# One more scheduling step in the S5 loop of a hybrid SSD / S5 / attention layer, and a higher pace for S5's steps

## The chip, the cores and the metric

The kernel runs on one core of one Trainium2 chip. The metric is the device time of one execution in microseconds (us). The kernel before took 1111.87 us, the median of three runs (1111.23, 1111.87 and 1114.11).

## The reference

One inference step of a layer with three branches. A prompt group (16 learned tokens and 512 prompt tokens) and a sample group (64 tokens on top of a cache of 512) go through the same weights. Cut to what matters:

```python
h = rmsnorm(x, norm_mix)                       # D_MODEL = 1024
y_a = ssd_branch(h @ w_z, h @ w_xbc, h @ w_dt) # conv, chunked scan, gate, group norm
y_b = s5_branch(h @ w_u)                       # complex diagonal scan, 32 groups x 64 states
glu = gelu(y_b) @ w_glu
out_b = glu[..., :1024] * sigmoid(glu[..., 1024:])
o_c = stick_breaking(rmsnorm(q), rmsnorm(k), v)
gates = sigmoid(h @ w_gate)                    # three gates of 1024 columns
mix = gates[0] * (y_a @ w_lift_a) + gates[1] * out_b + gates[2] * (o_c @ w_lift_c)
x = x + mix @ w_out
x = x + square(relu(rmsnorm(x) @ w_up)) @ w_down
```

In `s5_branch` the input of every group is mapped to complex states, a recurrence with a fixed complex factor runs over time, and the states are mapped back. The kernel does this in blocks of eight steps: products of powers of the factor with B (`ba_r`, `ba_i`), their product with C (`psk`, later the table `tz`), one scan over blocks, and a second product.

## The kernel before, in words

All large products are dense matmuls in three passes (L336 to L338: high part by high part, high by low, low by high), 128 weights wide, on column halves of 288 or 296. `dense()` walks the weight tiles one after another: for each half it takes one PSUM tile `ps_d`, issues its matmuls and evacuates it. Which engine evacuates depends on the product. In the stretch of `w_glu` (`ybx` is gelu(y_b)) each of eight tiles m has four halves: two of the gate, whose sigmoid ACT writes to `gls` (DVE multiplies it into `gt`), and two of the value, which DVE multiplies into `mix`. A half has 12 matmuls here and 24 in the other products. The weights come by DMA (`w_raw`) and are split by ACT into `w_hi` and by DVE into `w_lo`.

The smaller work (S5, attention, SSD) is written as generators, and each `yield` ends a step. After every half `side(kt)` adds the pace of the first generator in the list, times kt/8, to `credit`; for every whole credit it traces one step. When a generator ends, the next one goes on with the credit that is left:

```python
PACE = {"s5_parts": 1.25, "s5": 1.35, "attention": 1.8, "ssd": 1.1}
        def side(kt):
            credit[0] += pulls[0][1] * kt / 8 if pulls else 0.0
            while credit[0] >= 1.0:
                credit[0] -= 1.0
                pull()
```

The instructions of a step keep their traced order on each of DVE, ACT, POOL and TensorE (`in_order`), while the evacuations and weight splits have a raised priority. A scheduler with a timeline of its own then sets the final order of each engine, and also which PSUM slot a tile gets, and so whose reader it has to wait for.

S5 goes through a loop over q, eight times, with three steps each: `cmul` of `ba_r` and `ba_i` on DVE and POOL; then TensorE transposes them into `ps_r` (L764), adds to `psk` (L765), and ACT copies `ps_r` to `rr`; then `ps_bs` (L775) and the products `mo` on DVE. Behind the loop `kd` is made of `psk`, goes to memory (`kd_scr`, L797) and comes back as `tz` (L834), with which TensorE makes `ps_y` (L847). After S5 comes attention, then SSD, whose chunks c = 1 to 5 are worked on beside `w_glu`: `decay` (an exponential `a` on ACT, L1270; 16 small subtractions on DVE, L1272; an exponential `ar` on ACT, L1273), `weigh` (`ar` times `cb` on DVE), `outputs` (`ps_y`, 32 matmuls, L1318), `state` (`ps_st`, L1293), `turned` (`ps_bt`, `ps_x`), `gather` and `gated`. The sigmoid and the exponential belong to different tables of ACT, so that ACT loads a table (ACT_TABLE_LOAD) whenever it goes from one to the other.

Of the kernel before, what the change touches and what calls it, by code (L numbers as in the profile page):

```python
# [31 lines left out]
LEAD = 120  # L32
WARM = 14
SPLITS = 3
PACE = {"s5_parts": 1.25, "s5": 1.35, "attention": 1.8, "ssd": 1.1}
BUFS = {"ea": 3, "eb": 4, "ec": 3}

PA = {}
# [23 lines left out]
def mixed():  # L62
    n = dict.fromkeys("xzabc", 0)
    out = []
    for c in ORDER:
        out.append(({"x": "xbc", "z": "z", "a": "g1", "b": "g2", "c": "g0"}[c], n[c]))
        n[c] += 1
    return out
# [108 lines left out]
def body(tc, io):  # L177
# [6 lines left out]
    with ExitStack() as ctx:  # L184
# [31 lines left out]
        def tt(e, o, a, b, op):  # L216
            e.tensor_tensor(o, a, b, op=op)  # L217

        def cmul(e, p, shape, orr, oi, ar, ai, br, bi):
            n = 1  # L220
            for x in shape[1:]:
                n *= x
            t = []
            e = e if isinstance(e, tuple) else (e, e)
            for j in range(4):
                g = e[j // 2] is G
                x = p.tile([128, 256], F32, name="cm%d" % j, tag="cm%s%d" % (g, j))[:, :n]
                if len(shape) == 3:
                    x = x.rearrange("p (a b) -> p a b", b=shape[2])
                if len(shape) == 4:  # L230
                    x = x.rearrange("p (a b c) -> p a b c", b=shape[2], c=shape[3])
                t.append(x)
            tt(e[0], t[0], ar, br, OP.mult)
            tt(e[0], t[1], ai, bi, OP.mult)
            tt(e[1], t[2], ar, bi, OP.mult)
            tt(e[1], t[3], ai, br, OP.mult)
            tt(e[0], orr, t[0], t[1], OP.subtract)
            tt(e[1], oi, t[2], t[3], OP.add)
# [210 lines left out]
        def behind(ins, gen):  # L449

            while True:
                with tc.issue_after(ins):
                    if next(gen, done) is done:
                        return
                yield
# [70 lines left out]
        def do_qk(name, m, g, dst, parts):  # L526
            qs = etile("qs", "ea")
            sq = etile("qsq", "eb")
            sh = etile("qsh", "eb", dt=F32R)
            sl = etile("qsl", "ec", dt=F32R)  # L530
            rq = etile("rq", "ec")

            def evac(cols, ps):
                n = cols.stop - cols.start
                copied(cols, ps, qs)
                S.activation(sq[:, cols], ps, AF.Square)
                split(sq[:, cols], sh[:, cols], sl[:, cols])
                pn = psg.tile([128, 512], F32, name="ps_q", tag="g")
                PE.matmul(pn[:, :n], blkr, sh[:, cols], start=True, stop=False)
                PE.matmul(pn[:, :n], blkr, sl[:, cols], start=False, stop=True)  # L540
                rstd_of(ev, pn[:, :n], 64, rq[:, cols], n, "rs")
            dense((name, m), hh, hl, evac, parts=parts)
            c = slice(parts[0].start, T)
            V.scalar_tensor_tensor(qs[:, c], qs[:, c], g, rq[:, c], op0=OP.mult, op1=OP.mult)
            SP.dma_start(dst[m, :, c], qs[:, c])
# [43 lines left out]
        def do_dt():  # L589
            for cols in halves:  # L590
                ps = psd.tile([128, 512], F32, name="ps_dt", tag="d")
                p = ps[:32, :H]
                for k in range(8):
                    PE.matmul(p, w2[:, 0, k, :], hh[:, k, cols], start=k == 0, stop=False)
                    PE.matmul(p, w2[:, 1, k, :], hl[:, k, cols], start=False, stop=k == 7)
                S.activation(dtr[:, cols], p, AF.Copy)
# [123 lines left out]
        def s5():  # L720
# [30 lines left out]
            for q in range(8):  # L751
                ba_r = sp.tile([128, 2, 8, 16], F32, name="ba_r", tag="ba_r%d" % (q % 2))
                ba_i = sp.tile([128, 2, 8, 16], F32, name="ba_i", tag="ba_i%d" % (q % 2))
                sh = [128, 2, 8, 16]
                tq = slice(2 * q, 2 * q + 2)
                P = lambda x: x[:, 7::-1, tq].rearrange("p s t -> p t s").unsqueeze(3).to_broadcast(sh)
                BB = lambda x: x[:, tq, :].unsqueeze(2).to_broadcast(sh)
                cmul((V, G), sp, sh, ba_r, ba_i, P(pr), P(pi), BB(bb_r), BB(bb_i))
                yield
                ps = psg.tile([128, 512], F32, name="ps_r", tag="g")  # L760
                for t in range(2):
                    tq = 2 * q + t
                    for j, (ba, cd) in enumerate(((ba_r, cd_r), (ba_i, cd_i))):
                        PE.transpose(ps[:, 256 * j + 128 * t:256 * j + 128 * t + 128], fs(ba[:, t]), ident)  # L764
                        PE.matmul(psk[:, 32 * tq:32 * tq + 32], fs(ba[:, t]), fs(cd[:, tq]), start=j == 0, stop=j == 1,  # L765
                                  skip_group_check=True)
                rr = sp.tile([128, 512], F32, name="rr", tag="rr%d" % (q % 2))
                S.activation(rr, ps, AF.Copy)
                yield
                z = psg.tile([128, 512], F32, name="ps_bs", tag="g")  # L770
                for t in range(2):
                    for j in range(2):
                        for gl in range(2):
                            c0 = 256 * j + 128 * t + 64 * gl
                            PE.matmul(z[64 * gl:64 * gl + 64, (2 * j + t) * NX:(2 * j + t + 1) * NX],  # L775
                                      rr[:, c0:c0 + 64], ub[:, 2 * (2 * q + t) + gl, :],
                                      start=True, stop=True, skip_group_check=True)
                v3 = lambda x: x.rearrange("p (t b) -> p t b", b=NX)
                zr, zi = v3(z[:, 0:2 * NX]), v3(z[:, 2 * NX:4 * NX])
                ts = slice(2 * q, 2 * q + 2)  # L780
                er, ei = em_r[:, ts, :], em_i[:, ts, :]
                m = [sp.tile([128, 2, NX], F32, name="mo%d" % j, tag="mo%d" % j) for j in range(4)]
                tt(V, m[0], zr, er, OP.mult)
                tt(V, m[1], zi, ei, OP.mult)
                tt(V, m[2], zi, er, OP.mult)
                tt(V, m[3], zr, ei, OP.mult)
                tt(G, d_r[:, ts, :], m[0], m[1], OP.add)
                tt(G, d_i[:, ts, :], m[2], m[3], OP.subtract)
                yield
# [626 lines left out]

        pulls.append((behind(last.ins, s5_parts()), PACE["s5_parts"]))
        for m in range(4):
# [4 lines left out]
        n1.release()  # L1423
        do_dt()
        pulls.append((s5(), PACE["s5"]))
        for m in range(4):
            do_qk("q", m, qg, q_scr, live)
            do_v(m)
            do_qk("k", m, kg, io["k_out"], halves)
        pulls.append((attention(), PACE["attention"]))  # L1430
        for n, m in mixed():
            if n == "xbc":
                do_xbc(m)
                if m == 9:
                    pulls.append((ssd(), PACE["ssd"]))
            elif n == "z":
# [225 lines left out]
```

## Time and profile before

| what | value |
|---|---|
| median of three runs | 1111.87 us (1111.23 to 1114.11) |
| the profiled execution, its own time | 1113.19 us |
| its span | 1111.5 us |
| granted clock, mean over the span | 0.998 |
| TensorE matmul busy | 1095.5 us, 99% |
| TensorE weight load busy | 1056.3 us, 95% |
| VectorE busy | 795.7 us, 72% |
| ScalarE busy | 540.7 us, 49% |
| GpSimd busy | 125.4 us, 11% |

The span is what the profiler saw of the program; the profiled execution's own time has 1.7 us around it. Names: PE is TensorE, PEld its weight loads, DVE is VectorE, ACT ScalarE, POOL GpSimd, SPq the DMA queue of SyncE. L336 is line 336 of the kernel. A row of a timeline gives the start, the duration, the engine, the line, the operation, what it wrote and read, and how many such instructions the row holds; in brackets stands the idle time of the engine ahead of it and what ended that.

### The profile page before, as it was taken

The page shows a single profiled execution, that of the slowest core. Times are in us where ns is not written, and L with a number is a line of the kernel's source. Part 1 is how long each engine was busy: PE and PEld are TensorE (multiplying, and loading weights), DVE is VectorE, ACT ScalarE, POOL GpSimd, SP SyncE. Part 2 cuts the span into 40 slices and gives each one's busy share as a digit, 9 for nine tenths or more (in the row PEclk, how much of TensorE's full clock was granted, in tenths as well). Part 3 has the DMA queues.
Part 4 walks back from the last instruction along what each step waited for, and adds up shares of the span by engine and source line. Part 5 has one row for each costly group of instructions (what it writes and reads, how often), then busy time and mean ns, then how long its engine had stood idle before and what let it go on. Part 6 is the DMA issues. An engine that isn't in the chain of part 4 may idle for free.

```text
span 1111.5 us, 21286 instructions
## 1 busy us (share of the span) xinstructions
PE 1095.5 (99%) x8532; PEld 1056.3 (95%) x8532; DVE 795.7 (72%) x1390; ACT 540.7 (49%) x928; POOL 125.4 (11%) x193
## 2 busy tenths in 40 slices
PE   9999999999999999999999999999999999999998
PEld 8998999999998999897888999999999999999998
DVE  7968579965767466468989754477867776786787
ACT  6465466633365545365657333354444444444443
POOL 1087233011000000021310001200000000000000
PEclk9999999999999999999999999999999999999999
DMA  7653223566754353187445533222232223123222
GB/s 274 149 138 114 94 80 132 136 190 171 222 178 151 112 169 136 64 267 247 133 139 178 173 109 115 99 76 77 76 114 80 74 84 123 60 77 133 77 82 80
DMA packets 80594, 144.04 MB, mean 130 GB/s; under 512 B 26512, under 2 KB 40688, under 8 KB 79984
## 3 DMA queue, kind: packets, MB, share of 16 engines
q1 hardware_dynamic: 80496, 142.69, 41.7%
q8 instruction: 67, 1.10, 0.4%
q14 instruction: 31, 0.25, 0.1%
HBM read 117.40 MB, written 24.38 MB: 128 GB/s over the span
## 4 chain that ended last, share of the span: by engine, by line
PE 83%; DVE 8%; ACT 3%; POOL 2%; issue 2%; DMA 2%; SPq 1%; POOLq 0%; ACTq 0%; DVEq 0%
PE ps_d L336 19%; PE ps_d L337 19%; PE ps_d L338 18%; PE ps_x L1581 3%; PE ps_x L1580 3%; PE ps_x L1582 3%; PE ps_o L895 2%; PE ps_z L895 2%; PE ps_y L1581 1%; PE ps_y L1580 1%; PE ps_y L1582 1%; PE ps_y L1318 1%; DVE w_lo L217 1%; DVE ya L217 1%; PE ps_z L1581 1%
## 5 line engine op out<-in xcount | busy, mean ns | idle before, releaser
L253 ACT ACTIVATE w_hi<-w_raw 128x1024 fp32r<-128x1024 f32 (+1 forms) x150 | 151.9, 1012 | 219.8 <-PE ps_d L337 142.2
L336 PE MATMUL ps_d<-hh,w_hi 128*128 128x288 f32 (+1 forms) x864 | 258.2, 299 | 0.0
L337 PE MATMUL ps_d<-hl,w_hi 128*128 128x288 f32 (+1 forms) x864 | 258.0, 299 | 0.0
L338 PE MATMUL ps_d<-hh,w_lo 128*128 128x288 f32 (+1 forms) x864 | 258.0, 299 | 0.0
L217 DVE TENSOR_TENSOR w_lo<-w_raw,w_hi 128x1024 fp32r<-128x1024 f32 (+1 forms) x150 | 180.3, 1202 | 95.2 <-ACT w_hi L253 91.9
L337 PEld LDWEIGHTS ps_d<-hl,w_hi 128*128 128x128 f32 x864 | 162.6, 188 | 0.9 <-issue 0.3
L338 PEld LDWEIGHTS ps_d<-hh,w_lo 128*128 128x128 f32 x864 | 162.6, 188 | 0.6
L336 PEld LDWEIGHTS ps_d<-hh,w_hi 128*128 128x128 f32 x864 | 162.7, 188 | 0.2
L336 PE MATMUL ps_d<-x2h,w_hi 128*128 128x288 f32 x512 | 151.2, 296 | 0.0
L337 PE MATMUL ps_d<-x2l,w_hi 128*128 128x288 f32 x512 | 151.1, 295 | 0.0
L338 PE MATMUL ps_d<-x2h,w_lo 128*128 128x288 f32 x512 | 150.3, 295 | 0.0
L336 PEld LDWEIGHTS ps_d<-x2h,w_hi 128*128 128x128 f32 x512 | 96.2, 188 | 0.1
L338 PEld LDWEIGHTS ps_d<-x2h,w_lo 128*128 128x128 f32 x512 | 96.2, 188 | 0.1
L337 PEld LDWEIGHTS ps_d<-x2l,w_hi 128*128 128x128 f32 x512 | 96.2, 188 | 0.0
L253 ACT ACTIVATE w_hi<-ws 128x1024 fp32r<-128x1024 f32 x32 | 34.0, 1061 | 55.0 <-PE ps_y L1581 21.6
L1581 PE MATMUL ps_x<-ftl,w_hi 128*128 128x288 f32 x192 | 56.7, 295 | 0.5 <-DVE ftl L217 0.5
L1580 PE MATMUL ps_x<-fth,w_hi 128*128 128x288 f32 x192 | 56.8, 296 | 0.2 <-ACT s L1600 0.2
L1582 PE MATMUL ps_x<-fth,w_lo 128*128 128x288 f32 x192 | 56.4, 294 | 0.0
L1531 ACT ACTIVATE fr<-ps_d 128x288 f32<-128x288 f32 x64 | 25.7, 402 | 55.8 <-PE ps_d L338 55.8
L217 DVE TENSOR_TENSOR w_lo<-ws,w_hi 128x1024 fp32r<-128x1024 f32 x32 | 39.1, 1220 | 12.6 <-ACT w_hi L253 12.6
L336 PE MATMUL ps_d<-ybx,w_hi 128*128 128x288 f32 x128 | 39.7, 310 | 3.0 <-DVE mix L217 2.3
L906 DVE TENSOR_TENSOR_SCAN aw<-col,aw 128x400 f32<-128x400 f32 (+4 forms) x36 | 30.7, 898 | 16.6 <-ACT aw L250 16.6
(471 smaller groups left out, 2643.3 us busy)
## 6 DMA issues: line engine op xcount, KB each, us to landing
w_raw<-wts SPq DMA_DIRECT2D x150, 512.0 KB, 3.5
g_scr<-go SPq DMA_DIRECT2D x24, 288.0 KB, 2.8
gt<-g_scr SPq DMA_DIRECT2D x24, 288.0 KB, 3.0
ar<-ac_scr SPq DMA_DIRECT2D x4, 1024.0 KB, 7.5
x_scr<-cs SPq DMA_DIRECT2D x10, 297.5 KB, 3.1
xc<-x_scr SPq DMA_DIRECT2D x4, 640.0 KB, 7.4
xt<-xT SPq DMA_DIRECT2D x8, 296.0 KB, 5.6
z_scr<-zs SPq DMA_DIRECT2D x8, 288.0 KB, 5.0
```

What stands on the lines that cost most here:

```text
L217: e.tensor_tensor(o, a, b, op=op)
L253: S.activation(hi, x, AF.Copy)
L336: PE.matmul(ps, wh[:, c], xh[:, k, cols], start=start and k == 0, stop=False)
L337: PE.matmul(ps, wh[:, c], xl[:, k, cols], start=False, stop=False)
L338: PE.matmul(ps, wl[:, c], xh[:, k, cols], start=False, stop=stop and k == kt - 1)
L895: mm = lambda *a, **b: PE.matmul(*a, skip_group_check=True, **b)
L906: V.tensor_tensor_scan(x, one.to_broadcast([128, n]), x, 1.0, op0=OP.mult, op1=OP.mult)
L1318: PE.matmul(py[oo, 128 * (h // 2):128 * (h // 2) + n], a, b, start=step == 0, stop=step == 1, skip_group_check=True)
L1531: S.activation(r[:, cols], ps, AF.Relu)
L1580: PE.matmul(ps, w[0][:, o], fh[:, k], start=first and k == 0, stop=False, skip_group_check=True)
L1581: PE.matmul(ps, w[0][:, o], fl[:, k], start=False, stop=False, skip_group_check=True)
L1582: PE.matmul(ps, w[1][:, o], fh[:, k], start=False, stop=k == 3, skip_group_check=True)
```

## The change

The pace of S5's steps goes from 1.35 to 1.53, and a bare `yield` is added in the loop over q, between `cmul` and the transposes. A loop body has four steps instead of three, and S5 has 68 steps instead of 60. All lines from 760 on are one further down after the change.

```diff
-PACE = {"s5_parts": 1.25, "s5": 1.35, "attention": 1.8, "ssd": 1.1}
+PACE = {"s5_parts": 1.25, "s5": 1.53, "attention": 1.8, "ssd": 1.1}
...
                 cmul((V, G), sp, sh, ba_r, ba_i, P(pr), P(pi), BB(bb_r), BB(bb_i))
                 yield
+                yield
                 ps = psg.tile([128, 512], F32, name="ps_r", tag="g")
```

68/60 is 1.133, as is 1.53/1.35, so that S5's last step is traced at the same `side` call as before, and attention's steps are too. The credit left over is another one, by which three steps of SSD are traced one half earlier: the ninth (outputs and state of chunk 1), the twentieth (decay of chunk 5 and the first `gated`) and the thirty-first. The order of the engines differs in the S5 stretch, a little in attention's, and in the stretch of `w_glu`; from the `w_out` product on it is the same.

On ACT in the stretch of `w_glu`, from the first exponential of chunk 4 (`a_6029`) on, the order before was:

```order
L1270 ACTIVATE a_6029<-ar 64x1024 x2
L250 ACT_TABLE_LOAD
L250 ACTIVATE gls<-ps_d 128x288 x2
L253 ACTIVATE w_hi<-w_raw 128x1024
L250 ACTIVATE gls<-ps_d 128x288
L1273 ACT_TABLE_LOAD
L1273 ACTIVATE ar<-ar 128x2048
L1240 ACTIVATE bt<-ps_bt 64x128
L250 ACT_TABLE_LOAD
L250 ACTIVATE gls<-ps_d 128x288
```

At the same place on ACT after the change:

```order
L1271 ACTIVATE a_6029<-ar 64x1024 x2
L250 ACT_TABLE_LOAD
L250 ACTIVATE gls<-ps_d 128x288 x2
L1274 ACT_TABLE_LOAD
L1274 ACTIVATE ar<-ar 128x2048
L253 ACTIVATE w_hi<-w_raw 128x1024
L250 ACT_TABLE_LOAD
L250 ACTIVATE gls<-ps_d 128x288 x2
L1241 ACTIVATE bt<-ps_bt 64x128
```

The first `gls` of tile m = 3 stood ahead of the long exponential `ar`; now the exponential, the weight split `w_hi` and a table load stand ahead of it.

On TensorE the two gate halves of that tile m = 3 are `ps_d_7100` and `ps_d_7115` (names with their numbers). Before, the output block of chunk 3 (`ps_y_6076`, with `ps_st` and `ps_bt` behind it) stood between them:

```order
L336 MATMUL ps_d_7100<-ybx_3296,w_hi_6960 128x288
L337 MATMUL ps_d_7100<-ybx_3296,w_hi_6960 128x288
L338 MATMUL ps_d_7100<-ybx_3296,w_lo_6961 128x288
L1318 MATMUL ps_y_6076<-ar_5724,xd_5766 64x128 x4
L1318 MATMUL ps_y_6076<-a2_5816,st_5899 64x128 x4
```

After the change the second half follows the first at once, and the block stands behind it:

```order
L336 MATMUL ps_d_7100<-ybx_3296,w_hi_6960 128x288
L337 MATMUL ps_d_7100<-ybx_3296,w_hi_6960 128x288
L338 MATMUL ps_d_7100<-ybx_3296,w_lo_6961 128x288
L336 MATMUL ps_d_7115<-ybx_3296,w_hi_6960 128x288
L337 MATMUL ps_d_7115<-ybx_3296,w_hi_6960 128x288
L338 MATMUL ps_d_7115<-ybx_3296,w_lo_6961 128x288
```

In both programs `ps_d_7115` waits for the reader of `ps_d_7100`, the first `gls` of the tile.

On DVE, a little further on, before the change (`a_6243` belongs to the last chunk of decay, `mix` to the values of m = 3):

```order
L217 TENSOR_TENSOR cb<-ps_bt,cst 64x64 x2
L217 TENSOR_TENSOR gt<-gt,gls 128x288
L1272 TENSOR_SCALAR ar<-ar,acm 64x64 x16
L217 TENSOR_TENSOR a_6243<-a_6243,xc 128x8x64
L217 TENSOR_TENSOR ya<-ya,zl 128x288 x2
L217 TENSOR_TENSOR mix<-ps_d,gt 128x288
L217 TENSOR_TENSOR xd<-ps_x,dt 64x512 x2
L217 TENSOR_TENSOR ar<-ar,cb 128x1024 x2
```

And after it (the same last chunk is `a_6209` there):

```order
L217 TENSOR_TENSOR cb<-ps_bt,cst 64x64 x2
L217 TENSOR_TENSOR st<-st,bd 128x512
L217 TENSOR_TENSOR mix<-ps_d,gt 128x288 x2
L217 TENSOR_TENSOR xd<-ps_x,dt 64x512 x2
L217 TENSOR_TENSOR ar<-ar,cb 128x1024 x2
L1273 TENSOR_SCALAR ar<-ar,acm 64x64 x16
L217 TENSOR_TENSOR a_6209<-a_6209,xc 128x8x64
L217 TENSOR_TENSOR ya<-ya,zl 128x288 x2
```

The two `mix` stand ahead of the 16 small subtractions of the last chunk now, and behind them before.

## Rows read from the trace of the kernel before

**Rows 1.** The page: busy time and share of each engine; the chain's shares.
```profile
PE 1095.5 (99%) x8532; PEld 1056.3 (95%) x8532; DVE 795.7 (72%) x1390; ACT 540.7 (49%) x928; POOL 125.4 (11%) x193
...
PE 83%; DVE 8%; ACT 3%; POOL 2%; issue 2%; DMA 2%; SPq 1%; POOLq 0%; ACTq 0%; DVEq 0%
```

**Rows 2.** Waits of TensorE: us in total, times, the longest.
```profile
PE ps_d L336 <- DVE mix L217: 2.3, 3, 1.9
...
PE ps_d L336 <- DVE gt L217: 1.0, 1, 1.0
...
PE ps_ac L1184 <- DVE dta L217: 0.8, 1, 0.8
PE ps_r L764 <- POOL ba_i L217: 0.8, 1, 0.8
PE ps_n L408 <- DVE sa L217: 0.7, 2, 0.5
PE ps_d L336 <- ACT gls L250: 0.6, 1, 0.6
```

**Rows 3.** Windows: length, busy time (x instructions), clock, DMA share, GB/s.
```profile
110.00:217.00 107.00, 107.00 (x866) 104.47 (x866) 85.05 (x123) 62.99 (x141) 29.42 (x46) 1.00 0.36 109
...
515.00:535.00 20.00, 19.38 (x178) 16.39 (x176) 18.79 (x44) 14.31 (x14) 4.22 (x3) 1.00 0.54 169
535.00:555.00 20.00, 18.12 (x164) 15.02 (x163) 18.45 (x48) 13.92 (x18) 5.79 (x4) 0.98 0.39 113
...
554.04:557.45 3.41, 3.41 (x16) 3.41 (x16) 3.41 (x5) 1.89 (x4) 0.00 (x0) 0.50 0.16 44
```

**Rows 4.** Timeline, S5's last block product to the first use of tz.
```profile
190.39 0.75 PE L775 MATMUL ps_bs<-ub,rr 128*64 128x76 f32 x16
...
192.86 0.69 DVE L217 TENSOR_TENSOR kd<-psk,pb 128x512 f32<-128x512 f32 x1
...
193.57 4.06 SPq L797 DMA_DIRECT2D kd_scr<-kd  x8
200.59 7.34 SPq L834 DMA_DIRECT2D tz<-kd_scr  x16
...
206.24 0.34 PE L847 MATMUL ps_y<-ub,tz 128*128 128x73 f32 x2
```

**Rows 5.** Timeline of TensorE at the end of attention.
```profile
303.98 0.43 PE L1184 MATMUL ps_ac<-dta,cst 128*128 128x96 f32 x2 [0.81 <-DVE dta L217]
```

**Rows 6.** Timeline of ACT around the second exponential of chunk 4.
```profile
535.10 0.71 ACT L250 ACTIVATE gls<-ps_d 128x288 f32<-128x288 f32 x2
537.33 1.06 ACT L253 ACTIVATE w_hi<-w_raw 128x1024 fp32r<-128x1024 f32 x1 [1.52 <-PE ps_d L337]
539.05 0.41 ACT L250 ACTIVATE gls<-ps_d 128x288 f32<-128x288 f32 x1 [0.66 <-PE ps_d L338]
540.03 1.28 ACT L1273 ACT_TABLE_LOAD   x1 [0.57 <-DVE ar L1272]
541.33 1.91 ACT L1273 ACTIVATE ar<-ar 128x2048 f32<-128x2048 f32 x1
```

**Rows 7.** Timeline of TensorE: chunk 3's output block and the halves behind it.
```profile
538.95 0.71 PE L1318 MATMUL ps_y<-ar,xd 128*64 128x128 f32 x8
...
544.37 0.40 PE L336 MATMUL ps_d<-ybx,w_hi 128*128 128x288 f32 x1
...
553.75 0.40 PE L336 MATMUL ps_d<-ybx,w_hi 128*128 128x288 f32 x1 [1.88 <-DVE mix L217]
```

**Rows 8.** Timeline of DVE in the same stretch.
```profile
536.82 2.35 DVE L217 TENSOR_TENSOR ar<-ar,cb 128x1024 f32<-128x1024 f32 x2
539.08 0.87 DVE L1272 TENSOR_SCALAR ar<-ar,acm 128x128 f32<-128x128 f32 x4
...
548.65 3.34 DVE L1272 TENSOR_SCALAR ar<-ar,acm 64x64 f32<-64x64 f32 x16 [1.49 <-ACT a L1270]
...
553.26 0.44 DVE L217 TENSOR_TENSOR mix<-ps_d,gt 128x288 f32<-128x288 f32 x1
```

## The prediction, made before the change was timed

> **What bounds the kernel now.** I read the page's shares and its chain first, then the list of TensorE's waits, then windows over the stretches that the change moves, and last the timeline of single instructions there. The reader is to see in the shares that TensorE is busy 1095.5 of 1111.5 us and that the chain runs over it for 83% [rows 1]: 16 us of idle are all that any reordering can win. In the list of waits, no single place has more than 1.9 us [rows 2]. In the windows, the stretch of S5's loop from 110 to 217 us has TensorE busy for 107.00 of 107.00 us, so that nothing can be won there, whatever DVE and POOL do beside it [rows 3]. The one S5 wait in the list, 0.8 us for `ba_i`, lies before that stretch. The second half of the list is the stretch of `w_glu` and SSD: from 515 to 535 us DVE is busy 18.79 of 20 us, from 535 to 555 us 18.45, and TensorE falls to 18.12 there; right behind its longest wait the granted clock is 0.50, the lower level of 1.2 GHz, for 3.41 us [rows 3]. So the change has to be judged where S5 is not: in attention's end and in SSD, whose steps shift by a half.
>
> **The change part by part.** The sums go against the profiled execution's own time, 1113.19 us; the median of the runs shown is 1111.87, so 1.32 us come off at the end.
>
> The bare yield costs no instruction. It only moves the transposes and everything behind them in a loop body to later calls of `side`, while the higher pace brings them forward; a body took 3 steps / 1.35 = 2.22 halves and takes 4 / 1.53 = 2.61. TensorE's matmuls of S5 are the same ones, inserted at other places into a stream that was full. I take 0 for them. Bounds: a wait like the one for `ba_i`, 0.8 us [rows 2], once more or once less. That wait itself stays, since the order of TensorE is the same up to its place.
>
> The later part of the chain of S5 gets a little tighter. From the start of the last `ps_bs`, at 190.39, over `kd` (192.86), its way to memory (from 193.57) and the reload (from 200.59) to the first `ps_y` at 206.24 it is 15.9 us, and TensorE had no gap there [rows 3, 4]. By the order, both ends move forward by about two halves, and the distance on TensorE is some 4.5 halves where it was 4.6, about 15.5 us by the trace's pace; 15.9 - 15.5 makes a wait of 0.4 us. The instruction behind it on SP's queue is the store of the convolution's rows, which nothing waits for soon. Bounds: 0, if the reload's first transfer lands early, and 2, if the 7.34 us in which SPq issues its sixteen parts [rows 4] fall behind a weight load. I take 0.3.
>
> At attention's end TensorE waits 0.81 us for `dta` [rows 5]. In the changed order `ps_ac` stands 0.13 halves later, some 0.4 us, and the DVE chain ahead of it no later. I take -0.5, with bounds of -0.8 and 0.
>
> Now SSD. First, the 0.6 us that TensorE waits for `gls` [rows 2] lie at a place where ACT does `w_hi` ahead of an exponential; after the change it does it behind, one `w_hi` of 1.06 us [rows 6] less ahead of that `gls`. I take -0.5, bounds -0.6 and 0.
>
> Second, and the largest term: TensorE finished the first gate half of tile m = 3 when chunk 3's block began, at 538.95 us, and went on with the second half at 544.37 [rows 7]. That half needs the PSUM tile that `gls` reads, at 539.05 to 539.46 [rows 6]; 5.42 us of `ps_y`, `ps_st` and `ps_bt` hid it. After the change nothing lies between the halves, and on ACT a long exponential, a `w_hi` and two table loads stand ahead of that `gls`. How late is it? The exponential waits for the 16 subtractions of chunk 4 on DVE. They ended at 539.95 before [rows 8]; now the two products `ar<-ar,cb` (2.35 us) and one `xd` (some 0.6) come behind them, so they end at about 537.0. Then, with the durations of [rows 6], a table load 1.30, the exponential 1.91, `w_hi` 1.06, a table load 1.30, `gls` 0.41: 5.98 us, so TensorE goes on at about 543.0. It comes to this place 0.5 earlier than before by the term above, at 538.45. The wait is 543.0 - 538.45, some 4.5 us. The block now runs behind the second half, where it hides nothing that waits. I take +4.5. Bounds: +0.6, the wait for `gls` in the list [rows 2], and +5.4, if the subtractions end where they ended before but for the `xd` and one of the two products (0.87 us later than I reckon, the length of their last four [rows 8]).
>
> Here a page of the Trainium skill speaks. The trace shows that a table load of 1.28 us at 540.03 is followed by the exponential at 541.33, without a gap [rows 6]. The Trainium skill (ScalarE: Activation LUTs, section "What ACT_TABLE_LOAD costs") gives 1283 ns for the load, as this trace does, and about 1380 ns of a drain with every switch to another set. With that, two switches ahead of `gls` would make the wait 2.8 us longer and the sum as much higher; the row shows no such drain ahead of the exponential, so I follow the row.
>
> Third, the clock. A wait of 1.88 us is followed by 3.41 us at the lower level, [rows 3, 7]; half of that, 1.7, is lost. The waits of 0.8 to 1.0 us have no such price: the mean clock of the span, 0.998, is 2.2 us short of full speed in all, and this place alone makes 1.7 of it. A wait of 4.5 us is taken to bring the same as that of 1.88: +1.7, bounds 0 and 1.7.
>
> Fourth, the longest wait goes: 1.88 us for `mix` [rows 7]. There DVE had the 16 subtractions of the last chunk (3.34 us, itself held up 1.49 us by ACT) ahead of `mix` [rows 8]; after the change both `mix` stand ahead of the 16. With TensorE some 4 us later at that place, `mix` is there in time. The wait goes and its stretch at the lower clock too: -1.9 - 1.7 = -3.6. Bounds -3.6 and 0. What is late next is the 16 subtractions themselves, for which the last, small block waits; it comes several halves later.
>
> Fifth, behind it stand three waits for DVE: 1.0 for `gt`, 0.7 for `sa` and the rest of `mix`, 0.4, 2.1 us in all [rows 2]. There DVE is the bound, and its work is the same. If TensorE comes to them later, they shrink by as much. The loss so far in this stretch is -0.5 + 4.5 + 1.7 - 3.6 = +2.1; I take half of the waits, -1.0, bounds -2.1 and +1.0 (a `ps_n` is issued earlier in relation to `sa` in the new order).
>
> Sum: 0.3 - 0.5 - 0.5 + 4.5 + 1.7 - 3.6 - 1.0 = +0.9, so 1114.1 for the profiled execution and 1112.8 for the median. Less than 0.3%, 3.3 us, is what a measurement of this kernel cannot tell from no change, and this is a quarter of it.
>
> **The rivals.**
> *The new wait is not paid back: slower.* Place: the second gate half of m = 3. If `gls` is late by 4.5 us there, the `gt` product on DVE behind it is, too, and in a strict queue all that DVE has behind it: `mix`, `ya`, the state. The DVE windows have only 1.2 and 1.55 us of idle in 20 [rows 3], so what DVE loses there it does not win back, and TensorE waits for `mix` again. Then the term of -3.6 is missing and that of -1.0 too: +0.9 + 4.6 = +5.5, so 1117.4. It decides from the point where DVE idles more than some 2 us at that `gt`; less than that and `w_lo` and `ar<-ar,cb` fill the time. For it speaks how full DVE is, against it that these products now stand exactly ahead of the `gt`. By the drain of the Trainium skill's page this case would come nearer.
> *The new wait is short: faster.* If the exponential has been done before TensorE arrives (the subtractions end earlier, or the scheduler's order leaves ACT free), the wait is 0.6 like the other one for `gls` [rows 2], without a fall of the clock. Then 0.3 - 0.5 - 0.5 + 0.6 - 3.6 = -3.7 with nothing back from the waits behind; with half of them, 1.0, it is -4.7, so 1107.2. Against it: the exponential alone takes 1.91 us, and it can't start before the subtractions.
> *It does for S5 what its words suggest: it takes the waits for `ba_i` away.* That would be -0.8 in the sum, 1112.0. Against it, the order is unchanged where that wait lies. This ends within 0.3% as well.
>
> **How the numbers follow.** The forecast, within 3.3 us of 1111.87, gets 0.42, and the third rival another 0.03 within the same bounds. The slower rival gets 0.30, since two large terms lie on its side and DVE is nearly full there; the faster one gets 0.25, since the waits of SSD are all near the size of what DVE's order decides. The likeliest case alone runs from 1109.5 to 1115. For 8 in 10 the range goes to the other cases, down to the faster rival at 1107.5 and up almost to the slower one, 1117.
>
> **What would show it right or wrong.** In the changed kernel's profile: the wait for `mix` of 1.9 us and the clock of 0.50 behind it gone; in their place a wait of TensorE for `gls` of 4 to 5.4 us near 538 us, with the lower clock behind it; the waits for `gt` and `sa` near 584 to 604 smaller; S5's stretch full, with at most 0.4 us ahead of the first `ps_y`; `dta` at 0.3 or so. It would be wrong if the `gls` wait is under 2 us, if DVE has a gap of over 2 us behind it, or if S5's stretch shows more than 1 us of idle.

## The result, and the profile after

The change made the kernel slower: 1124.06 us (median of four runs, 1121.52 to 1124.46) against 1112.99 for the kernel before in the same sessions (four runs, 1111.23 to 1114.53). The ratio is 1.0085, with a 95% interval of 1.0061 to 1.0109. The forecast was 1112.8, with a range up to 1117. The profiled execution took 1123.75 us, 10.6 more than that of before.

The page's first part for the changed kernel, as [rows 1]: 

```profile
span 1121.9 us, 21287 instructions
...
PE 1097.7 (98%) x8532; PEld 1057.9 (94%) x8532; DVE 796.2 (71%) x1390; ACT 543.9 (48%) x931; POOL 127.6 (11%) x193
```

The work is the same and only three ACT instructions were added, all of them table loads (931 instead of 928). TensorE has 24 us of idle where it had 16. The list of its waits, which answers to [rows 2]:

```profile
PE ps_d L336 <- ACT gls L250: 7.7, 3, 3.4
PE ps_y L848 <- DMA tz<-kd_scr: 2.2, 2, 1.7
PE ps_ac L1185 <- DVE dta L217: 1.5, 1, 1.5
...
PE ps_n L408 <- DVE sa L217: 1.3, 1, 1.3
...
PE ps_r L765 <- POOL ba_i L217: 0.8, 1, 0.8
PE ps_d L336 <- DVE zs L217: 0.7, 1, 0.7
PE ps_r L765 <- DVE ba_r L217: 0.6, 1, 0.6
...
PE ps_d L336 <- DVE mix L217: 0.4, 1, 0.4
```

The long wait for `mix` (1.88 of the 2.3 us before) is gone, as forecast, and a wait for `gls` stands in its place, as forecast. But there are three of these, 7.7 us together, and S5 and attention have new waits for `tz`, `zs` and `ba_r` and a longer one for `dta`. The timeline of TensorE shows the largest four, with the idle time in brackets:

```profile
259.90 0.41 PE L848 MATMUL ps_y<-ub,tz 128*128 128x73 f32 x2 [1.65 <-DMA tz<-kd_scr]
...
526.78 0.40 PE L336 MATMUL ps_d<-ybx,w_hi 128*128 128x288 f32 x1 [1.62 <-ACT gls L250]
...
548.02 0.40 PE L336 MATMUL ps_d<-ybx,w_hi 128*128 128x288 f32 x1 [3.43 <-ACT gls L250]
...
599.72 0.40 PE L336 MATMUL ps_d<-ybx,w_hi 128*128 128x288 f32 x1 [2.64 <-ACT gls L250]
```

The windows (length, busy time of each engine, granted clock, DMA share, GB/s), as [rows 3], show what two of them cost beside the idle time:

```profile
170.00:190.00 20.00, 19.19 (x162) 18.32 (x162) 17.35 (x29) 8.70 (x23) 8.68 (x15) 1.00 0.37 125
250.00:270.00 20.00, 18.35 (x144) 18.14 (x143) 8.15 (x14) 5.93 (x11) 3.27 (x3) 1.00 0.66 173
290.00:312.00 22.00, 20.50 (x157) 20.29 (x156) 13.66 (x47) 8.32 (x17) 0.59 (x2) 1.00 0.77 229
...
544.00:556.00 12.00, 8.57 (x85) 5.71 (x83) 6.70 (x11) 4.35 (x5) 0.00 (x0) 0.86 0.21 70
...
597.00:605.00 8.00, 5.36 (x27) 5.00 (x27) 7.55 (x16) 6.09 (x10) 0.00 (x0) 0.79 0.43 130
```

A clock of 0.86 over 12 us and of 0.79 over 8 us is 1.7 us lost each time: after both long `gls` waits the clock was at its lower level for a while, after the one of 1.62 it was not (1.00 from 523 to 530 us).

The cleanest account comes from setting the start of each dense matmul of the changed kernel against the same one before. The lag is +4.9 us when SSD's stretch begins (389 us in the kernel before). At 557 us of the kernel before, where the `mix` wait and its lower clock are behind it, it is +7.0, and at 592 us it is +12.4; it ends at +10.5. So 4.9 us were lost in S5 and attention, 2.1 in SSD up to the `mix` place, and 3.5 behind it. In the first of these stretches the clock was 1.00 throughout, so that no part of the 4.9 is the lower clock's.

How the `gls` of tile m = 3 came to be late is read from ACT, as [rows 6]:

```profile
540.07 0.71 ACT L250 ACTIVATE gls<-ps_d 128x288 f32<-128x288 f32 x2
542.10 1.28 ACT L1274 ACT_TABLE_LOAD   x1 [1.31 <-DVE ar L1273]
543.39 1.92 ACT L1274 ACTIVATE ar<-ar 128x2048 f32<-128x2048 f32 x1
545.21 1.04 ACT L253 ACTIVATE w_hi<-w_raw 128x1024 fp32r<-128x1024 f32 x1
546.27 1.28 ACT L250 ACT_TABLE_LOAD   x1
547.56 0.41 ACT L250 ACTIVATE gls<-ps_d 128x288 f32<-128x288 f32 x1
```

From 542.10 to the end of `gls` at 547.97 it is 5.87 us; the prediction had 5.98 for this chain. The exponential follows its table load at 543.39 with no gap, and the second load follows `w_hi` at 546.27 with none either. The Trainium skill (ScalarE: Activation LUTs, "What ACT_TABLE_LOAD costs") has about 1380 ns of a drain with every switch to another set; these rows do not agree.

The third wait was not forecast. It is in the last tile, whose first gate half TensorE ran from 591.42 to 593.18 us. On ACT ahead of the `gls` that reads it:

```profile
592.77 1.28 ACT L243 ACT_TABLE_LOAD   x1
594.07 0.50 ACT L243 ACTIVATE rsl<-ps_n,col 128x288 f32<-128x288 f32 x1
594.59 1.28 ACT L244 ACT_TABLE_LOAD   x1
595.88 0.45 ACT L244 ACTIVATE sa<-rsl 128x288 f32<-128x288 f32 x1
596.23 1.04 ACT L253 ACTIVATE w_hi<-w_raw 128x1024 fp32r<-128x1024 f32 x1
...
597.96 1.28 ACT L250 ACT_TABLE_LOAD   x1
599.25 0.71 ACT L250 ACTIVATE gls<-ps_d 128x288 f32<-128x288 f32 x2
```

The logarithm (L243) and the exponential (L244) of the SSD norm each load a table, then the sigmoid does. ACT has no gap from 591.89 on. The first load begins 0.4 us before TensorE's half ends, and three loads, 3.84 us, lie between that half and its `gls`.

### The profile page after: what moved, and what is told of

The parts are those of the page before. It is cut to its first block, busy times and chain, and to the rows that moved or that the text cites. A ratio compares the mean times of both kernels' runs of the same rounds, so it can differ in the third digit from the quotient of the medians.

```text
span 1121.9 us, 21287 instructions
## 1 busy us (share of the span) xinstructions
PE 1097.7 (98%) x8532; PEld 1057.9 (94%) x8532; DVE 796.2 (71%) x1390; ACT 543.9 (48%) x931; POOL 127.6 (11%) x193
## 4 chain that ended last, share of the span: by engine, by line
PE 79%; DVE 8%; ACT 4%; DMA 3%; POOL 3%; SPq 2%; issue 2%; DVEq 0%; ACTq 0%; POOLq 0%
PE ps_d L336 18%; PE ps_d L337 18%; PE ps_d L338 17%; PE ps_x L1582 3%; PE ps_x L1581 3%; PE ps_x L1583 3%; PE ps_o L896 2%; PE ps_z L896 2%; PE ps_y L1582 1%; PE ps_y L1581 1%; PE ps_y L1319 1%; PE ps_y L1583 1%; POOL cm L217 1%; DVE w_lo L217 1%; ACT w_hi L253 1%
```

## The experiments

Theory 1: two separate losses. One is in S5 and attention, whose order the yield and the pace change; the other is in SSD, whose steps come a half earlier through the credit that is left over, and it is made of table switches on ACT. Rivals: all of it is in one of the two, or the second only follows from the first. Fourteen kernels were run; each was timed in turns with the kernel before, which stood between 1113.2 and 1114.2 us in these sessions.

**The two halves apart.** e1 is the kernel before with SSD's steps traced early, e2 the changed kernel with SSD's steps traced as before. The order of every engine in e1 is that of the kernel before up to the end of attention and that of the changed kernel from there; in e2 it is the other way round.

```diff
 # e1: before, e2: after, at the start of ssd()
+            credit[0] += 0.105      # e1
+            credit[0] += -0.095     # e2
```

> The kernel before with 0.105 added to the credit when SSD begins: S5 and attention keep their order, and SSD's stretch has exactly the order of the changed kernel. In the traces the changed kernel is 4.8 us behind the kernel before when SSD's stretch begins and 10.5 us at the end. Theory 1 (two separate losses, one in S5 and attention, one in SSD): +5.7 us, no more tz wait than before, gls waits of 1.7, 3.4 and 2.8 us with two stretches at the lower clock. Rival, the SSD loss only comes with S5's new order: 0 to +1. Rival, SSD is all of it: +10.

> The changed kernel with 0.095 taken from the credit when SSD begins: S5 and attention keep the changed order, SSD's stretch has exactly the order of the kernel before. Theory 1: +4.8 us, made up of waits for tz (2.2), dta (0.7 more), zs (0.7) and ba_r (0.6); SSD's waits those of before (mix 1.9). Rival, the reordering of S5 costs nothing (as predicted): within 1 us of the kernel before. Rival, all of the loss is in S5: +10.

Measured: e1 1120.01 against 1113.5, ratio 1.0066 (1.0049 to 1.0084), +6.5 us by the medians; e2 1117.74, ratio 1.0042 (1.0028 to 1.0055), +4.2. Together 10.7 us: by the medians the two losses add up to the change's (11.1), and neither rival holds. The waits in e1 are

```profile
PE ps_d L336 <- ACT gls L250: 8.4, 3, 3.4
...
PE ps_n L408 <- DVE sa L217: 1.3, 1, 1.3
```

and in e2, with `mix` back and `gls` as small as before,

```profile
PE ps_d L336 <- DVE mix L217: 2.4, 3, 2.0
PE ps_y L848 <- DMA tz<-kd_scr: 1.6, 2, 0.9
...
PE ps_ac L1185 <- DVE dta L217: 1.4, 1, 1.4
...
PE ps_r L765 <- DVE ba_r L217: 0.6, 1, 0.6
```

In e1's profile the lag was already +1.3 at the end of attention, with an order equal to that before, so that SSD's part is 4.3 there. The largest piece of it is a stretch at the lower clock, 1.7 us lost, with no wait of TensorE right before it; against that, the wait of 0.8 for `dta` is missing. The three `gls` waits, 2.34, 3.40 and 2.65 us in this profile, have no such stretch behind them:

```profile
277.30:280.71 3.41, 3.41 (x17) 3.41 (x16) 2.90 (x11) 1.36 (x2) 0.00 (x0) 0.50 0.87 269
500.00:610.00 110.00, 99.41 (x893) 85.23 (x891) 92.04 (x205) 69.19 (x90) 18.34 (x11) 1.00 0.55 170
```

So SSD's loss does not need the lower clock. The clock also explains how far S5's part varies. The five profiles of kernels with S5's old order (e1, e3, e4, e6, e8) are 1.3, 3.5, -0.3, 3.1 and 0.2 us behind the kernel before at the end of attention. Without what the lower clock took there (1.7, 3.4, 0, 3.4 and 0) it is between -0.4 and +0.2. With the new order it is 4.9 in the changed kernel, 3.7 in e2 and, without 1.7, 4.1 in e5: the new order itself costs some 4 us.

**Which step of SSD.** e3 and e4 trace one step early each (`k` is 9 or 20). The thirty-first moves nothing: e4, without it, has the order of e1 behind 561 us (567 in e1's time).

```diff
+        def one_early(gen, k):
+            for i, _ in enumerate(gen):
+                credit[0] += 0.105 if i == k - 1 else -0.105 if i == k else 0.0
+                yield
...
-                    pulls.append((ssd(), PACE["ssd"]))
+                    pulls.append((one_early(ssd(), 9), PACE["ssd"]))
```

> The kernel before with only the ninth step of SSD (outputs and state of chunk 1) traced a half earlier. Theory 1: this step brings the waits for gls near 525 and 544 us and takes away the one for mix: 1.1 + 3.4 + 1.7 (clock) - 1.9 - 1.7, about +2.6 by 570 us; behind that the order is a third one, and no trace shows it: 0 to +5 in all. Rival, the step of chunk 5's decay carries all: 0.

> The kernel before with only the twentieth step of SSD (decay of chunk 5 and the first gated) traced a half earlier. Theory 1: the waits near 525 and 544 us do not appear, the wait for mix at 551 stays or shrinks, and the late wait for gls near 597 us (2.8 and a stretch at the lower clock, 1.7) appears: +3 to +5. Rival, the late wait only follows from the lateness that the first step brings: 0.

Measured: e3 1116.22, ratio 1.0026 (1.0012 to 1.0041), +2.7; e4 1113.55, ratio 1.0003 (0.9993 to 1.0013). The first step does bring the first two waits for `gls`, 0.95 and 3.44 us, and takes away the long one for `mix`. The +2.7 is not its price, though: in the trace 3.5 us of lag were there at the end of attention, of which the lower clock made 3.4, and SSD added 1.1. For e4 the total agrees with the rival and the trace with the theory: by 580 us it is 4.3 us ahead of the kernel before, relative to where it entered SSD's stretch, since the `mix` wait and its low clock are gone, and by 592 us it has lost that and 1.5 more; behind that it gains again and ends at +0.4:

```profile
PE ps_d L336 <- ACT gls L250: 3.3, 2, 2.6
...
PE ps_n L408 <- DVE sa L217: 1.3, 1, 1.3
```

So the wait of 2.64 us belongs to the second step and does not need the first; e3 has a shorter one, 1.45 us, at its own late place. By the traces the two steps alone cost 1.1 and 0.4 us, and 4.3 to 5.7 together. The reason, as reckoned from the rows: each of them takes away the `mix` wait with its lower clock, 3.6 us, and together they can do it only once.

**Table loads.** The gates' sigmoid is written as a tanh, which needs no other table than the exponential. TensorE's order stays word for word the same in all three; ACT loads 22 tables, where the changed kernel has 36 and the kernel before 33.

```diff
-                sigmoid(ps, s[:, cols])
-                tt(V, g[:, cols], g[:, cols], s[:, cols], OP.mult)
+                S.activation(s[:, cols], ps, AF.Tanh, scale=0.5)
+                V.scalar_tensor_tensor(g[:, cols], s[:, cols], 1.0, g[:, cols], op0=OP.add, op1=OP.mult)
...
-                tt(V, mix[:, m, cols], ps, g[:, cols], OP.mult)
+                V.scalar_tensor_tensor(mix[:, m, cols], ps, 0.5, g[:, cols], op0=OP.mult, op1=OP.mult)
```

> The changed kernel with the sigmoid of the w_glu gates written as a tanh (0.5 * (1 + tanh(x/2)), the sum and the factor in the DVE products that are there anyway). TensorE's order is unchanged; ACT loads 22 tables instead of 36, since the gates then need no other table than SSD's exponentials. Theory 1 (the table loads ahead of gls are what makes the three gls waits so long): one load of 1.28 us less ahead of the gate near 525 us, two near 544, one near 597, and the two stretches at the lower clock (1.7 each) go with the waits: -5 to -8 us against the changed kernel, so about 1117. Rival (the exponential and the DVE chain ahead of it set the time, the loads hide beside them): -1 at most.

> The same edit in the kernel before: TensorE's order unchanged, 22 table loads instead of 33. Theory 1: the exponential on which chunk 5's subtractions wait comes 1.28 us earlier or more, the wait for mix at 551 us falls from 1.9 to under 0.7 and the clock stays up: -3 to -4 us. Rival (DVE alone sets that wait): within 1 us of the kernel before.

> e4 (only chunk 5's decay a half earlier) with the tanh. In e4's trace 4.6 us were won at the mix wait by 580 us and lost again to the waits for sa and gls at 577 to 586 with the lower clock. Theory 1 (table loads make the late gls wait): one load less there, 2.6 falls to 1.3 or less and the clock stays up: 3 us under e4, 1110 to 1111. Rival: as e4, 1113.

Measured: e5 (the change) 1114.70, ratio to the kernel before 1.0018 (1.0002 to 1.0034), 9.4 us under the change's median; e6 (the kernel before) 1112.72, ratio 0.9994 (0.9982 to 1.0006); e8 (e4) 1111.27, ratio 0.9981 (0.9969 to 0.9993). In e5 the waits for `gls` shrank from 7.7 to

```profile
PE ps_d L336 <- ACT gls L1463: 1.9, 2, 1.2
```

and on ACT the chain at tile m = 3 is now

```profile
541.34 1.92 ACT L1274 ACTIVATE ar<-ar 128x2048 f32<-128x2048 f32 x1 [1.84 <-DVE ar L1273]
543.16 1.04 ACT L253 ACTIVATE w_hi<-w_raw 128x1024 fp32r<-128x1024 f32 x1
544.11 0.39 ACT L1463 ACTIVATE gls<-ps_d 128x288 f32<-128x288 f32 x1
```

3.16 us instead of 5.87, two loads less. So what the early steps cost is almost all table switches: without them the change's SSD is 2.4 us ahead of that of before in the traces, counted from the end of attention, where it was 5.7 behind. Of the 2.4, 1.7 is the lower clock that the profile of before has behind its `mix` wait. The rival (loads hidden) falls for the change. For the kernel before the theory's second part falls: its `mix` wait stayed,

```profile
PE ps_d L336 <- DVE mix L1466: 2.4, 3, 1.9
```

because there DVE itself, with the 16 subtractions ahead of `mix`, sets the time: its wait for ACT in front of them fell from 1.49 to 0.32 us, but the 16 took 4.57 us instead of 3.34, for which no run here shows the cause. In e8 both go together, the order without the `mix` wait and the gates without switches, and TensorE is busy for 20.00 of 20 us from 540 to 560 us:

```profile
540.00:560.00 20.00, 20.00 (x203) 15.37 (x200) 18.46 (x45) 7.02 (x11) 6.23 (x5) 1.00 0.37 99
```

e8 is the only kernel here that beats both, by 1.9 us against the kernel before.

**The S5 half: the reload of `tz`.** Four kernels test whether the two buffers or the eight DMAs make the waits; the third buffer shares its place with `rr0`. e7 and e13 build on e2, e11 on the kernel before and e12 on e8.

```diff
 # e7, e11, e12
-                tz = sp.tile([128, 4, 128], F32, name="tz", tag="tz%d" % (it % 2))
+                tz = sp.tile([128, 4, 128], F32, name="tz", tag=("tz0", "tz1", "rr0")[it % 3])
 # e13
-                for s in range(8):
-                    SP.dma_start(tz[16 * s:16 * s + 16, :, :], kv[:, gs, (7 - s) * 16:(7 - s) * 16 + 128])
+                SP.dma_start(tz, kd_scr[0:512, 0:128].rearrange("(p a) b -> p a b", a=4))
```

> e2 (the change, with SSD as before) with a third buffer for tz. Theory 1 (S5's steps behind the loop over q come at pace 1.53, 1.96 halves per round instead of 2.22, and two tz buffers can't be reloaded that fast): the waits for tz of 1.6 to 2.2 us go, so -1.5 to -2 against e2, about +2.5 against the kernel before. Rival (the transfers themselves are slow, whatever buffer they land in): within 0.5 of e2.

> e2 with each tz loaded by one DMA from a plain block of the same scratch tensor instead of eight with overlapping rows (so S5's second product gets other numbers; the instructions on TensorE are the same ones). Attention and SSD keep e2's order. Theory 1 (the reload of tz, eight DMAs on SP's queue, costs S5 its part): no tz wait, and e2's +4.2 falls by 1.5 to 3. Rival (S5's part is in DVE's order: ba_r, zs, dta): e2's time within 0.8 us, +3.5 to +4.2.

> The kernel before with a third buffer for tz. In profiles of kernels with S5's old order, tz waits of 0.3 to 1.8 us came and went, so the reload has no slack there either. Theory 1: median 0.5 to 1 us under the kernel before from S5; SSD's order also changes, by 0 to +5. Rival (the transfers are slow in any buffer): S5 unchanged.

> e8 (chunk 5's decay a half earlier, tanh gates: faster than both kernels) with the third tz buffer. SSD's order changes with it in the scheduler. Theory 1: without table switches the order in SSD costs less, so 1109 to 1112. Rival (the order of SSD decides with or without table loads): 1113 or more.

Measured: e7 1117.15, ratio 1.0036 (1.0020 to 1.0052), 0.6 under e2's median (0.3 when each is set against its own kernel before) and within its interval; its `tz` waits are 0.8 instead of 1.6, and its trace is 2.4 us behind at the end of attention where e2's is 3.7. e13 1117.21, ratio 1.0034 (1.0019 to 1.0049), and it still waits:

```profile
PE ps_y L847 <- DMA tz<-kd_scr: 1.9, 3, 1.3
```

So neither the third buffer nor one DMA in place of eight gives S5's loss back; the buffers are at most a small part of it, and the number of DMAs is not what makes the waits. What S5 would cost with no wait for `tz` at all, neither shows. e11 took 1125.78 (ratio 1.0109, 1.0092 to 1.0125) and e12 1117.26 (nine executions; a tenth took 3086; 1.0036, 1.0019 to 1.0053): both lose 6 us in S5 at once, half of it in

```profile
PE ps_y L849 <- DMA xs<-x_i: 3.2, 1, 3.2
```

and most of the rest at the lower clock right behind it, 3.4 us in e11 and 2.7 in e12:

```profile
222.79:229.62 6.83, 6.77 (x30) 6.77 (x31) 6.25 (x10) 3.08 (x9) 0.00 (x0) 0.50 0.85 257
```

In e11, with a free buffer, 24 parts of `tz` instead of 16 stand together at the head of SP's one queue, and a weight load comes right ahead of the states' copy. The copy is issued 0.9 us later than before and takes 8.3 us to land instead of 3.9. SSD's order came out different from that of before and of e8, though the buffer was all that was edited.

**The S5 half: yield and pace.** Theory 1 now says that the higher pace squeezes the later loop, with the `tz` reloads, too much; theory 2 that the extra yield moves the end of the loop over q forward on TensorE, and the reload with it. e9 is e2 with the extra yield in the loop of the `ps_y` products in place of the loop over q, e10 the yield with the old pace, e15 the pace without the yield.

```diff
-PACE = {"s5_parts": 1.25, "s5": 1.53, "attention": 1.8, "ssd": 1.1}   # e10
+PACE = {"s5_parts": 1.25, "s5": 1.35, "attention": 1.8, "ssd": 1.1}
...
                 cmul((V, G), sp, sh, ba_r, ba_i, P(pr), P(pi), BB(bb_r), BB(bb_i))
                 yield
-                yield                                                 # e9, e15
...
                 tt(V, oc, oc, od, OP.add)
                 yield
+                yield                                                 # e9
```

> e2 with the extra yield taken out of the loop over q and put into the loop of the eight ps_y products, behind the load of tz; pace 1.53 and 68 steps as in the change. SSD's order comes out different again, so only the trace up to the end of attention counts. Theory 1 (the loop over q was stretched and the later loop squeezed, from 2.22 to 1.96 halves per round, so the reload of tz is late): no tz wait over 0.5 and no wait for ba_r; under 1.5 us behind the kernel before at the end of attention. Rival (a higher pace anywhere delays DVE's other work): 3 us or more behind there, as the change.

> The change with the old pace of 1.35: the extra yield alone. S5 ends six halves later, attention and SSD with it, so the total is not comparable in its parts. Theory 1: the later loop has the old spacing, so the tz waits are those of before, under 0.6 us, though the loop over q is stretched more than in the change. Rival (the extra yield in the loop over q makes the tz waits): 1.5 us or more.

> The change without the extra yield: pace 1.53 alone, 60 steps, so S5 ends five halves earlier and SSD's order is another one. With e10 (yield alone) this is the fourth corner. Theory 2 (the yield moves the end of the loop over q forward on TensorE, to 41.0 halves in e10 and 42.7 in the change, where before and this kernel have 44.6 and 45.0; the tz reload follows it): no tz wait over 0.6 us here. Theory 1 (the pace makes the later loop too quick for two tz buffers): tz waits of 1.5 us or more.

Measured: e9 1132.27 (ratio 1.0171, 1.0151 to 1.0190), e10 1119.84 (1.0054, 1.0033 to 1.0075), e15 1130.03 (1.0145, 1.0126 to 1.0164). The `tz` waits of e10 and e15 are

```profile
PE ps_y L848 <- DMA tz<-kd_scr: 2.4, 4, 1.4
```

and

```profile
PE ps_y L847 <- DMA tz<-kd_scr: 5.7, 2, 4.9
```

Theory 1 fails by e10, where the old pace has as long `tz` waits as the change, and theory 2 by e15, where there is no extra yield. In e9 the `tz` waits stay under 0.5 each, as theory 1 had it, and yet it is some 13 us behind from 250 us on. In e9 and e15 the clock is 0.50 for 13.65 and 10.24 us around 237 us, beside waits of 2.3 and 5.0; TensorE was busy for 10.27 and 6.19 us of that, so 5.1 and 3.1 us were lost. In both corners SSD's order is another one too, so the totals are not S5's alone. What can be said is that the kernel before is the best of four corners: the yield without the pace costs 5.7 us, the pace without the yield 16.2, both together 11.1.

## Why the prediction was wrong

*S5's matmuls, 0, with a bound of 0.8: wrong.* "A stream that was full" was read as if it bounded the loss, but it told nothing of how far DVE and the reloads were behind it. From 170 to 312 us the changed kernel has about 5.4 us of idle on TensorE where before there was 1.1, which is one of the prediction's own signs of being wrong (more than 1 us). e2 puts the price of S5 and attention, all terms together, at 4.2 us (3.1 to 6.1 by its interval) where the prediction had 0 + 0.3 - 0.5. This is the first step that failed. The fully busy window [rows 3] says that nothing can be won, not that nothing can be lost: e6 has the order of before there and waits 1.3 us for `tz` in three places, so the reloads had little slack before the change.

*The reload, +0.3, bounds 0 to 2: the place was wrong, and the size.* The wait was forecast ahead of the first `ps_y`, at the end of the chain over `kd`. In the changed kernel the first `ps_y`, at 200.32, has no wait; the two that came, 2.2 us, are at later reloads (223.75 and 259.90), which the prediction did not look at.

*`dta`, -0.5: the wrong sign.* The wait grew from 0.81 to 1.50.

*The wait for `gls` near 522 us, -0.5: wrong, and by misreading the order.* `w_hi` moved behind the exponential `a`, but stayed ahead of this `gls`; beside that, `a` waited for its DMA. The wait went from 0.62 to 1.62.

*The wait at tile m = 3, +4.5: right, 1.1 too long.* 3.43 was measured, with the chain on ACT as reckoned (5.87 against 5.98); TensorE came to it later than reckoned, by what the earlier wait had cost. Its low clock, +1.7: right in this profile, but e1 has the same wait of 3.40 without it. The end of the `mix` wait and its low clock, -3.6: right. Up to there the prediction had +2.1 for SSD, and the lag between 389 and 557 us grew by 2.1: that is luck, since the failed and the mis-sized terms cancel there.

*What stands behind it, -1.0, bounds -2.1 and +1.0: wrong.* The wait for `gt` went, but `sa` rose from 0.7 to 1.3, and a `gls` wait of 2.64 with another stretch at the lower clock came, +3.5 in the lag. This is the second step that failed. The order of ACT was read at one place and taken as settled behind it. e4 shows that this wait comes with the second of the three early steps, of which the prediction priced only the moved subtractions.

*The rivals.* The slower one had its price (+5.5) near SSD's loss, and the wrong place: DVE idled 1.26 us at that `gt`, under the 2 us from which this rival counted, and did not hand the delay on there (its 4.04 us of idle at 555.36 is for TensorE's own block); ACT did by further switches. No rival had a loss in S5 as well.

*Left open:* why the extra yield makes S5's part slower. It moves the end of the loop over q some two halves forward on TensorE (from 44.6 to 42.7); what follows is spread over `ba_r`, `tz`, `zs` and `dta`, and no experiment took more than 0.9 us of it away by the medians, which the intervals do not tell from nothing.

## What to carry to other kernels

A table of paces that shares one left-over credit couples all stages behind it: 0.1 of a credit moved three steps by a half and cost 6.5 us, with nothing in that stage edited. Take such a coupling out first, as e1 and e2 do, before judging the edit itself. Where an engine that evacuates PSUM also switches function tables, every reorder can put two or three loads between a product and its reader; one set of functions for both (here the tanh) made the same reorder harmless in e5. And before a lag in one profile is put down to an order, take off what the clock cost in it: e3's lag in S5, 3.5 us with nothing changed there, was almost all the clock's.

## What was not expected of the hardware

The granted clock did not follow the waits from profile to profile. It fell to its lower level, for 3.41 us and 1.7 us of loss each time, after waits of 1.88 (before), 1.95 (e2), 2.64 and 3.43 us (the change). In e1's profile it did not fall after 2.34, 3.40 and 2.65 us, nor in e6's after 1.94. In e1, e3 and e6 it fell near 278 us, with no wait of more than 0.4 us close by; in e6 it stayed there for 6.83 us:

```profile
276.53:283.36 6.83, 6.83 (x30) 6.75 (x30) 3.89 (x18) 1.80 (x3) 0.00 (x0) 0.50 0.74 196
500.00:610.00 110.00, 105.59 (x932) 90.37 (x931) 100.45 (x213) 57.20 (x86) 20.33 (x12) 1.00 0.57 178
```

Executions of one kernel differ by it as well. Of 87 executions of the kernel before in these sessions, 41 have a mean clock of 0.998 like the profiled one and a median of 1113.5 us, and 21 have 0.999 or 1.000 and take 1110.5 to 1112.6. A table load of 1.28 us is followed by the next ACT instruction at once, in every case read here but those in which that instruction waited for something else (1.32 us for a DMA at 521.78 in the changed kernel). S5's reloads gave TensorE from 0 to 1.8 us of wait in kernels whose S5 order is the same; in the profile of e3 the reload's wait of 1.82 came with 3.5 us of lag, since two stretches at the lower clock, at 258.90 and 279.38 us, lay around it.
